# 256 rows of a rank scatter move from the SBUF path to row copies that GpSimd issues

## The chip, the cores and the metric

The kernel runs on one core of a Trainium2 chip. The metric is the device time of one execution in microseconds. The kernel before was timed three times; a separate execution was recorded by the hardware profiler, and all rows below are from that one.

## The reference

```python
B, N, D = 8, 2048, 2560
order = np.argsort(scores, axis=1)
ranks = np.argsort(order, axis=1)
out = np.zeros_like(x)
b_idx = np.arange(B)[:, None]
out[b_idx, ranks, :] = x
```

Each of 8 batches has 2048 rows of 2560 float32 values (10,240 bytes). A row's rank is the number of scores of its batch that come before its own, and the row is copied unchanged to that place in the output. So 168 MB are read and 168 MB are written, and nothing is computed on them; only the ranks are computed, from 64 KB of scores.

## The kernel before

**Ranks.** TensorE spreads the scores of a batch over all partitions (`broadcast`), VectorE counts for each row how many scores are smaller (`ranks`, the counting at line 317), and the sums become integer row numbers in `rank_i`. This goes batch by batch, in steps listed in `STEPS`.

**Groups of 256 rows through SBUF.** A batch has 8 groups of 256 rows; partition p of a group holds rows 2p and 2p+1. `BULK` lists the groups that go through SBUF. GpSimd issues all their transfers on one software queue: for group k one load into buffer k mod 8 (`load`: an indirect one at line 152, a plain one at line 165) and two scatters of 128 rows each (`scatter`, line 495). In the loop at the end GpSimd waits until the scatters of group k-4 are done, issues the load of group k+4, waits for load k and for the ranks of k, and issues the scatters of k. So some eight buffers are always between load and scatter, and the order of issue on GpSimd is the order of its queue.

**Rows that never enter SBUF.** Other rows are copied from HBM to HBM, one DMA for each row, since the target is known only as a number in a register. SyncE and ScalarE issue these DMAs on two hardware queues (`copy_rows`): a table of byte offsets is read into registers 32 at a time (line 446), then one DMA is issued for each row (line 456). `part` cuts the row into 2 x 2 pieces of 2,560 bytes, so that it runs on two of the core's 16 DMA engines. These rows are: all 256 of each group in `FULL`, half of the one in `HALF`, and *holes*.

**Holes.** In most groups some partitions are left out of load and scatter (`THIN`): their row numbers are pushed beyond the bounds, and the indirect DMA skips them. `WIDE_HOLE` is partitions 0 to 7 of 59 groups (16 rows each); `EXTRA` adds four partitions in four groups. For each distinct set of holes VectorE forms one column of `thin_row` at the start (reductions at lines 274 and 283); the first indirect load waits for it (`t_thin`). Before a buffer's first load with a hole, its partitions 0 to 7 are filled with zeros (`spare`: five times by ScalarE at line 217, once by GpSimd at line 511), so that nothing unwritten is read. In all 808 + 808 rows go through the two hardware queues.

**Offsets.** `rows_to_psum` turns ranks into one row with TensorE (line 378) and `to_bytes` makes byte offsets of them (line 389): for a copied group right after its ranks, for holes one batch later.

Of the kernel before, what the change touches and what calls it, by code (L numbers as in the profile page):

```python
# [7 lines left out]
P = 128  # L8
# [5 lines left out]
ENG = mybir.EngineType  # L14
# [26 lines left out]
def kernel(  # L41
# [6 lines left out]
    nc = tc.nc  # L48
    B, N, D = x.shape
    C = N // P  # L50
    ROW = 4 * D
# [2 lines left out]


    GROUPS = [(256 * i, 2) for i in range(8)]
    FULL = ((0, 0), (1, 0))
    HALF = ((2, 0),)
    MMAX = max(m for _, m in GROUPS)
    BULK = [(b, g) for b in range(B) for g in range(len(GROUPS)) if (b, g) not in FULL]  # L60
    NBUF = 8
# [1 line left out]


    PRIMED = {2: 'pool', 3: 'act', 4: 'act', 5: 'act', 6: 'act', 7: 'act'}
    WIDE_HOLE = (0, 8)
    EXTRA = {20: ((48, 4),), 30: ((44, 4),), 36: ((48, 4),), 52: ((48, 4),)}
    WHOLE = ()
    THIN = {
        key: (WIDE_HOLE, *EXTRA.get(k, ()))  # L70
        for k, key in enumerate(BULK)
        if key not in HALF and (k in PRIMED or k >= NBUF) and k not in WHOLE
    }

    HOLES = sorted(set(THIN.values()))
# [13 lines left out]
    def first_col(g):  # L89
# [9 lines left out]
    ident = pool.tile([P, P], F32, name="ident")  # L99
# [3 lines left out]
    rank = pool.tile([P, B * C], F32, name="rank")  # L103
# [4 lines left out]
    thin_row = pool.tile([P, len(HOLES)], I32, name="thin_row")  # L108
    copied = {k: 2 if k in FULL else 1 for k in FULL + HALF}
    full_i = {  # L110
        k: pool.tile([1, m * P], I32, name=f"full_i{k[0]}_{k[1]}") for k, m in copied.items()
    }
    thin_of = {b: [k for k in THIN if k[0] == b] for b in range(B)}
    thin_at = {}
    thin_n = {b: 0 for b in range(B)}
    for k, parts in THIN.items():
        thin_at[k] = thin_n[k[0]]
        thin_n[k[0]] += 2 * sum(n for _, n in parts)
    thin_i = {b: pool.tile([1, n], I32, name=f"thin_i{b}") for b, n in thin_n.items() if n}
    xb = [pool.tile([P, MMAX * D], F32, name=f"x{i}") for i in range(NBUF)]  # L120
    ps_all = psum.tile([P, N], F32, name="ps_all")
# [4 lines left out]
    out_bytes = out.rearrange("b n d -> (b n d)").bitcast(U8)  # L126
    x_bytes = x.rearrange("b n d -> (b n d)").bitcast(U8)

    with tc.tile_critical(no_gpsimd_drain=True):
        sp = Line(nc, nc.sync, "sp")  # L130
        act = Line(nc, nc.scalar, "act")
        pl = Line(nc, nc.gpsimd, "pool")
        dve = Line(nc, nc.vector, "dve")
# [3 lines left out]
        s_load = [nc.alloc_semaphore(f"load{i}") for i in range(NBUF)]  # L137
        s_scat = [nc.alloc_semaphore(f"scat{i}") for i in range(NBUF)]
        s_rows = {sp: nc.alloc_semaphore("rows_sp"), act: nc.alloc_semaphore("rows_act")}
        n_scat = [0] * NBUF  # L140

        n_load = [0] * NBUF
# [2 lines left out]
        def load(line, k, sem):  # L145
# [24 lines left out]
            if k:  # L170
# [13 lines left out]
                out=ident[:],  # L184
                in_=ident[:],
# [8 lines left out]
        for half in range(2):  # L194
# [3 lines left out]
                    out=part,  # L198
                    in_=part,
# [7 lines left out]


        def spare(k):
            return xb[k % NBUF][:WIDE_HOLE[1], :]  # L210

        t_primed = {}
        act.after(pl, t_ident)
        for k, who in PRIMED.items():
            if who == "act":
                t_primed[k] = act, act.did(
                    nc.scalar.copy(  # L217
                        out=spare(k),
                        in_=ident[:WIDE_HOLE[1], P - 1:].to_broadcast([WIDE_HOLE[1], MMAX * D]),
                    )  # L220
                )

# [3 lines left out]
        for g, (r, m) in enumerate(GROUPS):  # L226
            for j in range(m):
# [3 lines left out]
                        out=ps_col[:, B * c:B * (c + 1)],  # L231
                        in_=s_in[:, r + j:r + m * P:m],
# [6 lines left out]
                out=s_col[:].rearrange("p c b -> p (c b)"), in_=ps_col[:, :B * C]  # L239
# [6 lines left out]
        def broadcast(b):  # L246
            pe.after(dve, t_copied)
            ticks = []
            for c in range(C):
# [12 lines left out]
        t_rows = {}  # L262
# [5 lines left out]
                out=below[:], in_=mask[:, MMAX, :], axis=mybir.AxisListType.X, op=OP.add  # L268
            )
        )  # L270
        for i, parts in enumerate(HOLES):
            for n, (first, width) in enumerate(parts):
                dve.did(
                    nc.vector.tensor_reduce(
                        out=edge[:, n:n + 1],
                        in_=ident[:, first:first + width],
                        axis=mybir.AxisListType.X,
                        op=OP.add,
                    )
                )  # L280
            dve.after(dve, dve.n)
            dve.did(
                nc.vector.tensor_reduce(
                    out=hole[:, i:i + 1],
                    in_=edge[:, :len(parts)],
                    axis=mybir.AxisListType.X,
                    op=OP.add,
                )
            )
            dve.after(dve, dve.n)  # L290
        dve.did(
            nc.vector.tensor_scalar(
                out=hole[:], in0=hole[:], scalar1=float(N), scalar2=None, op0=OP.mult
# [6 lines left out]
                    out=thin_row[:], in0=hole[:], scalar1=below[:], scalar2=None, op0=OP.add  # L300
# [82 lines left out]
                    )  # L383
            dve.after(pe, pe.n)

        def to_bytes(out, b, g, first, n, m=2):
            lo = first_col(g)
            return dve.did(
                nc.vector.tensor_scalar(  # L389
                    out=out.rearrange("o (j i) -> o j i", j=m),  # L390
                    in0=ps_row[:1, P * lo:P * (lo + m)].rearrange("o (j p) -> o j p", j=m)[
                        :, :, first:first + n
                    ],
                    scalar1=float(b * N),
                    scalar2=float(ROW),
                    op0=OP.add,
                    op1=OP.mult,
                )
            )

        def thin_to_bytes(b):
            if thin_of[b]:
                rows_to_psum(thin_of[b])
            for k in thin_of[b]:
                at = thin_at[k]
                for first, width in THIN[k]:
                    t_rows[b] = to_bytes(
                        thin_i[b][:, at:at + 2 * width], b, k[1], first, width
                    )
                    at += 2 * width  # L410

        for b in range(B):
            dve.after(dve, dve.n)
            for q in range(4):
# [3 lines left out]
                        out=s_all[:, 512 * q:512 * (q + 1)],  # L418
                        in_=ps_all[:, 512 * q:512 * (q + 1)],
# [42 lines left out]
        def row_of(b, g, j, p):  # L462
            return b * N + GROUPS[g][0] + 2 * p + j

        for b in range(B):
            jobs = []
            for g in range(len(GROUPS)):
                if (b, g) in copied:
                    rows = [row_of(b, g, j, p) for j in range(copied[b, g]) for p in range(P)]
                    jobs.append((full_i[b, g], rows, t_rows[b, g]))  # L470
            rows = [
                row_of(b, g, j, p)
                for _, g in thin_of[b]
                for first, width in THIN[b, g]
                for j in range(2)
                for p in range(first, first + width)
            ]
            if rows:
                jobs.append((thin_i[b], rows, t_rows[b]))
            for table, rows, tick in jobs:  # L480
                half = len(rows) // 2
                copy_rows(sp, ENG.SP, b, table, 0, rows[:half], tick)
                copy_rows(act, ENG.Activation, b, table, half, rows[half:], tick)
# [4 lines left out]
        def scatters_done(line, k):  # L488
            line.wait(s_scat[k % NBUF], 16 * n_scat[k % NBUF])

        def scatter(k, j):
            b, g = BULK[k]
            col = b * C + first_col(g) + j
            n_scat[k % NBUF] += 1
            nc.gpsimd.indirect_dma_start(  # L495
                out=out_flat,
                out_offset=bass.IndirectOffsetOnAxis(ap=rank_i[:, col:col + 1], axis=0),
                in_=xb[k % NBUF][:, j * D:(j + 1) * D],
                in_offset=None,
                element_offset=b * N * D,  # L500
                **(dict(bounds_check=N - 1, oob_is_err=False) if (b, g) in THIN else {}),
            ).then_inc(s_scat[k % NBUF], 16)

        def load_ahead(k):
            i = k % NBUF
            load(pl, k, s_load[i])
            loaded[k] = (s_load[i], 16 * n_load[i])

        for k in range(1, NBUF):
            if PRIMED.get(k) == "pool":  # L510
                t_primed[k] = pl, pl.did(nc.gpsimd.memset(spare(k), 0.0))  # L511
            if k in t_primed:
                pl.after(*t_primed[k])
            load_ahead(k)
        for k, (b, g) in enumerate(BULK):
            if k >= LAG and k + NBUF - LAG < len(BULK):
                scatters_done(pl, k - LAG)
                load_ahead(k + NBUF - LAG)
            pl.wait(*loaded[k])
            pl.after(dve, t_bulk[b, g])  # L520
            for j in range(copied.get((b, g), 0), GROUPS[g][1]):
                scatter(k, j)
        for k in range(max(0, len(BULK) - NBUF), len(BULK)):
            scatters_done(pl, k)

        nc.gpsimd.dma_reset()

# [29 lines left out]
```

## Time and profile before

| | |
|---|---|
| median of 3 runs | 761.94 us (761.61 to 762.33) |
| the profiled execution | 761.48 us, of which the span is 759.8 us |
| busy share of the span | VectorE 55%, GpSimd 25%, TensorE 7%, ScalarE 3% |
| DMA queues: share of 16 engines | software queue 93.0%, hardware queues 3.8% and 2.9% |
| HBM | 177.83 MB read, 177.77 MB written |

The share of a DMA queue is the sum of the times of its packets over 16 times the span. A packet is one piece of data, or the 4 bytes by which a transfer reports that it is done. Packets that follow each other on one engine may overlap slightly in these records, so shares can add up to a little over 1.

### The profile page before, as it was taken

How to read it: one execution, taken by the hardware profiler on the slowest of the kernel's cores; microseconds unless marked ns; L12 is line 12 of the kernel's file. 1: busy time of each engine (PE TensorE's matmuls, PEld its weight loads, DVE VectorE, ACT ScalarE, POOL GpSimd, SP SyncE). 2: the span in 40 equal slices, each digit the busy share in tenths (PEclk: the TensorE clock that was granted, in tenths of full speed). 3: DMA queues.
4: the chain of work that ended last, by engine and by line, in shares of the span. 5: the costliest groups of instructions: out<-in, count | busy, mean ns of one | idle time of the engine just before them, and what ended most of it. 6: DMA issues, size and time to landing. Idle time of an engine off the chain costs nothing.

```text
span 759.8 us, 5293 instructions
## 1 busy us (share of the span) xinstructions
PE 55.3 (7%) x268; PEld 40.6 (5%) x268; DVE 419.9 (55%) x957; ACT 23.2 (3%) x6; POOL 189.6 (25%) x194
## 2 busy tenths in 40 slices
PE   3101001203003003003001002000000000000000
PEld 3101000102002002002000001000000000000000
DVE  6999998998998997998998990000000000000000
ACT  9200000000000000000000000000000000000000
POOL 5224222221321313133131322213131322312210
PEclk8555555555555555556555556555555555555555
DMA  8999999999999999999999999999999999999996
GB/s 360 427 412 427 423 422 427 424 421 433 424 422 429 426 431 424 429 428 424 428 424 431 426 428 428 426 430 425 431 423 431 424 429 426 425 427 425 421 406 292
DMA packets 36647, 319.43 MB, mean 420 GB/s; under 512 B 7664, under 2 KB 7664, under 8 KB 14128
## 3 DMA queue, kind: packets, MB, share of 16 engines
q0 software_dynamic: 26624, 299.84, 93.0%
q1 hardware_dynamic: 5136, 10.97, 3.8%
q10 hardware_dynamic: 4848, 8.28, 2.9%
q14 instruction: 37, 0.30, 0.1%
q8 instruction: 2, 0.03, 0.0%
HBM read 177.83 MB, written 177.77 MB: 468 GB/s over the span
## 4 chain that ended last, share of the span: by engine, by line
DMA 47%; DVE 42%; issue 3%; PE 3%; POOL 2%; POOLq 0%; SPq 0%
DMA out_dram<-x,rank_i 41%; DVE trash L317 36%; DMA x<-in_x_dram,thin_row 6%; PE ps_row L378 2%; DVE s_all L417 2%; DVE rank_i L364 1%; POOL out_dram L495 1%; DVE thin_i L389 0%; POOL x L152 0%; DVE rank_i L355 0%; DMA s_in<-in_scores_dram 0%; DVE rank L349 0%; DVE rank L343 0%; PE ps_row L230 0%; DVE full_i L389 0%
## 5 line engine op out<-in xcount | busy, mean ns | idle before, releaser
L317 DVE TENSOR_SCALAR_CACHE_REDUCE trash<-s_all,s_col 128x1792 bf16<-128x1792 f32 (+7 forms) x240 | 315.2, 1348 | 4.6
L152 POOL DMA_INDIRECT x<-in_x_dram,thin_row x59 | 61.3, 1039 | 445.3 <-DMA out_dram<-x,rank_i 262.5
L495 POOL DMA_INDIRECT out_dram<-x,rank_i x123 | 120.6, 981 | 86.2 <-issue 36.4
L317 DVE SCALAR_TENSOR_TENSOR trash<-s_all,s_col,mask 128x256 bf16<-128x256 f32 x128 | 61.6, 481 | 0.0
L378 PE MATMUL ps_row<-ident,rank 128*1 128x128 f32 x124 | 26.0, 390 | 343.4 <-DVE rank_i L364 287.3
L378 PEld LDWEIGHTS ps_row<-ident,rank 128*1 128x1 f32 x124 | 13.2, 113 | 355.5 <-DVE rank_i L364 290.0
L251 PE MATMUL ps_all<-ident,s_col 128*128 128x128 f32 x128 | 27.6, 405 | 58.3 <-DVE s_all L417 58.0
L251 PEld LDWEIGHTS ps_all<-ident,s_col 128*128 128x128 f32 x128 | 25.5, 219 | 60.6 <-DVE s_all L417 60.0
L217 ACT COPY x<-ident 8x5120 f32<-8x5120 f32 x5 | 21.9, 4453 | 0.0
L417 DVE COPY s_all<-ps_all 128x512 f32<-128x512 f32 x32 | 20.0, 684 | 0.3
L317 DVE DVE_READ_ACCUMULATOR trash<-s_all,s_col 128x1 f32 x240 | 19.9, 83 | 0.0
L389 DVE TENSOR_SCALAR thin_i<-ps_row 1x16 int32<-1x16 f32 (+1 forms) x63 | 5.7, 153 | 25.0 <-PE ps_row L378 25.0
L364 DVE TENSOR_SCALAR rank_i<-rank,hole 128x2 int32<-128x2 f32 x59 | 13.9, 236 | 2.1
L317 DVE DVE_READ_ACCUMULATOR trash<-s_all,s_col,mask 128x1 f32 x128 | 10.6, 83 | 0.0
L511 POOL MEMSET x<- 8x5120 f32 x1 | 4.4, 4354 | 0.0
L165 POOL DMA_DIRECT2D x<-in_x_dram x2 | 1.5, 736 | 8.6 <-DMA out_dram<-x,rank_i 8.6
L355 DVE CAST rank_i<-rank 128x4 int32<-128x4 f32 (+3 forms) x17 | 3.1, 185 | 0.6
L349 DVE TENSOR_TENSOR rank<-rank,acc 128x4 f32<-128x4 f32 (+3 forms) x17 | 2.8, 167 | 0.6
L343 DVE TENSOR_TENSOR rank<-acc,acc 128x4 f32<-128x4 f32 (+3 forms) x17 | 2.8, 166 | 0.6
L238 DVE COPY s_col<-ps_row 128x128 f32<-128x128 f32 x1 | 0.3, 292 | 4.8 <-PE ps_row L230 4.8
L230 PE MATMUL ps_row<-ident,s_in 8*128 8x8 f32 x16 | 2.1, 261 | 4.0 <-DMA s_in<-in_scores_dram 4.0
L389 DVE TENSOR_SCALAR full_i<-ps_row 1x256 int32<-1x256 f32 (+1 forms) x3 | 1.1, 368 | 2.0 <-PE ps_row L378 2.0
(16 smaller groups left out, 7.4 us busy)
## 6 DMA issues: line engine op xcount, KB each, us to landing
out_dram<-in_x_dram SPq DMA_DIRECT2D x808, 10.0 KB
out_dram<-in_x_dram ACTq DMA_DIRECT2D x808, 10.0 KB
x<-in_x_dram SPq DMA_DIRECT2D x1, 2560.0 KB, 12.7
x<-in_x_dram POOLq DMA_DIRECT2D x1, 2560.0 KB
out_dram<-x,rank_i POOLq DMA_INDIRECT x123
x<-in_x_dram POOLq DMA_DIRECT2D x1, 1280.0 KB, 40.5
x<-in_x_dram,thin_row POOLq DMA_INDIRECT x59, 41.4
s_in<-in_scores_dram SPq DMA_DIRECT2D x1, 64.0 KB
```

Of the source, the lines that this page charges most:

```text
L152: nc.gpsimd.indirect_dma_start(out=xb[k % NBUF][:, :m * D], out_offset=None, in_=x.rearrange("b (q j) d -> (b q) (j d)", j=m), in_offset=b ...
L217: nc.scalar.copy(out=spare(k), in_=ident[:WIDE_HOLE[1], P - 1:].to_broadcast([WIDE_HOLE[1], MMAX * D]),)
L251: nc.tensor.transpose(out=ps_all[:, P * c:P * (c + 1)], in_=s_col[:, c, b:b + 1].to_broadcast([P, P]), identity=ident[:],)
L317: do(out=trash[i][:, :P * (hi_c - lo_c)], in0=s_all[:, P * lo_c:P * hi_c], accum_out=acc[i][:, col:col + 1], **how,)
L343: nc.vector.tensor_tensor(out=rank[:, cols], in0=acc[0][:, cols], in1=acc[1][:, cols], op=OP.add)
L355: nc.vector.tensor_copy(out=rank_i[:, cols], in_=rank[:, cols])
L364: nc.vector.tensor_scalar(out=rank_i[:, cols], in0=rank[:, cols], scalar1=hole[:, i:i + 1], scalar2=None, op0=OP.add,)
L378: nc.tensor.transpose(out=ps_row[:1, P * c:P * (c + 1)], in_=rank[:, b * C + c:b * C + c + 1], identity=ident[:],)
L389: nc.vector.tensor_scalar(out=out.rearrange("o (j i) -> o j i", j=m), in0=ps_row[:1, P * lo:P * (lo + m)].rearrange("o (j p) -> o j p", j= ...
L417: nc.vector.tensor_copy(out=s_all[:, 512 * q:512 * (q + 1)], in_=ps_all[:, 512 * q:512 * (q + 1)],)
L495: nc.gpsimd.indirect_dma_start(out=out_flat, out_offset=bass.IndirectOffsetOnAxis(ap=rank_i[:, col:col + 1], axis=0), in_=xb[k % NBUF][:, ...
L511: t_primed[k] = pl, pl.did(nc.gpsimd.memset(spare(k), 0.0))
```

## The change

Group 4 of batch 1 (256 rows) leaves `BULK`, which now has 61 groups. Its rows are copied from HBM to HBM by GpSimd: one DMA for each row, a contiguous run of 10,240 bytes that is cut over all 16 DMA engines, 640 bytes on each. They go on GpSimd's software queue, six behind the scatters of a group, from group number 12 on; the offsets are read into GpSimd's registers 18 at a time. At the end GpSimd also waits for these rows.

A hole may now have a step (always 1 here). Groups 3, 4 and 5 of batch 0 (numbers 2, 3 and 4 of `BULK`) get a second hole, partitions 32 to 39, whose rows go to SyncE and ScalarE; `spare` fills 40 partitions in place of 8. The four older extra holes keep their numbers in `BULK`, and so three of them stand in the next group than before. The hardware queues now have 1,648 rows in place of 1,616.

```diff
-    FULL = ((0, 0), (1, 0))
+    FULL = ((0, 0), (1, 0), (1, 4))
     HALF = ((2, 0),)
+    BY_POOL = ((1, 4),)
+    POOL_FIRST, POOL_ROWS, POOL_LOADED = 12, 6, 18
...
-    WIDE_HOLE = (0, 8)
-    EXTRA = {20: ((48, 4),), 30: ((44, 4),), 36: ((48, 4),), 52: ((48, 4),)}
+    PRIMED_TO = 40
+    WIDE_HOLE = (0, 8, 1)
+    EXTRA = {2: ((32, 8, 1),), 3: ((32, 8, 1),), 4: ((32, 8, 1),), 20: ((48, 4, 1),), 30: ((44, 4, 1),), 36: ((48, 4, 1),), 52: ((48, 4, 1),)}
...
         def spare(k):
-            return xb[k % NBUF][:WIDE_HOLE[1], :]
+            return xb[k % NBUF][:PRIMED_TO, :]
...
-                if (b, g) in copied:
+                if (b, g) in copied and (b, g) not in BY_POOL:
                     rows = [row_of(b, g, j, p) for j in range(copied[b, g]) for p in range(P)]
                     jobs.append((full_i[b, g], rows, t_rows[b, g]))
...
+        pool_todo = [
+            (b, g, n, row_of(b, g, n // P, n % P))
+            for b, g in BY_POOL
+            for n in range(copied[b, g] * P)
+        ]
...
+        def pool_rows():
+            for b, g, n, row in pool_todo[:POOL_ROWS]:
+                pl.after(dve, t_rows[b, g])
+                if not pool_at:
+                    _, at = nc.values_load_multi_w_load_instructions(
+                        full_i[b, g][:, n:min(n + POOL_LOADED, copied[b, g] * P)],
+                        engines=[ENG.Pool],
...
+                    )
+                    pool_at.extend(at)
+                nc.gpsimd.dma_start(
+                    out=out_bytes[bass.ds(pool_at.pop(0), ROW)],
+                    in_=x_bytes[bass.ds(row * ROW, ROW)],
+                ).then_inc(s_pool_rows, 16)
+            del pool_todo[:POOL_ROWS]
...
             for j in range(copied.get((b, g), 0), GROUPS[g][1]):
                 scatter(k, j)
+            if k >= POOL_FIRST:
+                pool_rows()
+        assert not pool_todo
         for k in range(max(0, len(BULK) - NBUF), len(BULK)):
             scatters_done(pl, k)
+        pl.wait(s_pool_rows, 16 * pool_n)
```

## Rows read from the trace of the kernel before

**Rows 1.** The page: the span, and the DMA engines' busy tenths in 40 slices.
```profile
span 759.8 us, 5293 instructions
DMA  8999999999999999999999999999999999999996
```

**Rows 2.** Windows view: stretches from start and end; DMA share 1.00 means 16 engines.
```profile
core 0: us, PE busy (x) PEld busy (x) DVE busy (x) ACT busy (x) POOL busy (x), PEclk, DMA share, GB/s
4.00:20.00 16.00, 8.42 (x45) 7.84 (x46) 12.74 (x29) 16.00 (x5) 8.02 (x5) 0.81 1.01 429
200.00:400.00 200.00, 21.77 (x101) 15.59 (x102) 184.55 (x416) 0.00 (x0) 51.24 (x51) 0.53 1.01 427
...
735.00:750.00 15.00, 0.00 (x0) 0.00 (x0) 0.00 (x0) 0.00 (x0) 0.00 (x0) 0.50 0.97 400
750.00:754.00 4.00, 0.00 (x0) 0.00 (x0) 0.00 (x0) 0.00 (x0) 0.00 (x0) 0.50 0.89 376
754.00:757.00 3.00, 0.00 (x0) 0.00 (x0) 0.00 (x0) 0.00 (x0) 0.00 (x0) 0.50 0.30 126
757.00:760.00 3.00, 0.00 (x0) 0.00 (x0) 0.00 (x0) 0.00 (x0) 0.00 (x0) 0.50 0.03 10
```

**Rows 3.** The page: the chain that ended last, shares of the span by engine.
```profile
DMA 47%; DVE 42%; issue 3%; PE 3%; POOL 2%; POOLq 0%; SPq 0%
```

**Rows 4.** The page: DMA queues; packets, bytes, share of 16 engines' span.
```profile
q0 software_dynamic: 26624, 299.84, 93.0%
q1 hardware_dynamic: 5136, 10.97, 3.8%
q10 hardware_dynamic: 4848, 8.28, 2.9%
q14 instruction: 37, 0.30, 0.1%
```

**Rows 5.** Timeline of GpSimd, one late group: start, duration, what, idle before.
```profile
637.01 1.04 POOL L152 DMA_INDIRECT x<-in_x_dram,thin_row  x1 [8.59 <-DMA out_dram<-x,rank_i]
638.35 0.98 POOL L495 DMA_INDIRECT out_dram<-x,rank_i  x1 [0.30 <-issue]
639.64 0.97 POOL L495 DMA_INDIRECT out_dram<-x,rank_i  x1 [0.30 <-issue]
649.19 1.03 POOL L152 DMA_INDIRECT x<-in_x_dram,thin_row  x1 [8.57 <-DMA out_dram<-x,rank_i]
```

**Rows 6.** Tile view of the output: row copies; ns min/median/max, first and last start.
```profile
L456 SPq DMA_DIRECT2D out_dram<-in_x_dram x808: 613/631/2077, 20.5 to 742.7; - x162
L456 ACTq DMA_DIRECT2D out_dram<-in_x_dram x808: 623/633/2000, 20.6 to 748.0; - x162
```

**Rows 7.** The page: groups of instructions; busy us, mean ns, idle before.
```profile
L165 POOL DMA_DIRECT2D x<-in_x_dram x2 | 1.5, 736 | 8.6 <-DMA out_dram<-x,rank_i 8.6
L389 DVE TENSOR_SCALAR full_i<-ps_row 1x256 int32<-1x256 f32 (+1 forms) x3 | 1.1, 368 | 2.0 <-PE ps_row L378 2.0
L511 POOL MEMSET x<- 8x5120 f32 x1 | 4.4, 4354 | 0.0
```

**Rows 8.** Lines view: groups that the page leaves out; the same columns.
```profile
L274 DVE TENSOR_REDUCE edge<-ident 128x1 f32<-128x8 f32 (+1 forms) x5 | 0.6, 153 | 0.1
L180 POOL MEMSET mask<- 128x512 f32 x1 | 0.5, 528 | 0.0
```

**Rows 9.** View of line 446: offsets into registers; ns min/median/max.
```profile
L446 SPq TENSOR_LOAD <-full_i x10: 2065/4258/6757, 18.4 to 371.3; - x10
```

**Rows 10.** The page: DMA issues, the last number us from issue to landing.
```profile
x<-in_x_dram,thin_row POOLq DMA_INDIRECT x59, 41.4
```

**Rows 11.** Timelines: a scatter that waited for ranks, and ranks and scatters around 110 us.
```profile
37.90 0.96 POOL L495 DMA_INDIRECT out_dram<-x,rank_i  x1 [9.33 <-DVE rank_i L364]
...
109.58 0.75 DVE L364 TENSOR_SCALAR rank_i<-rank,hole 128x2 int32<-128x2 f32 x3
...
118.91 0.98 POOL L495 DMA_INDIRECT out_dram<-x,rank_i  x1 [0.30 <-issue]
```

More of the change, by code (lines that the diff above doesn't have):

```diff
@@ L65 @@
     PRIMED = {2: 'pool', 3: 'act', 4: 'act', 5: 'act', 6: 'act', 7: 'act'}
-    WIDE_HOLE = (0, 8)
-    EXTRA = {20: ((48, 4),), 30: ((44, 4),), 36: ((48, 4),), 52: ((48, 4),)}
+    PRIMED_TO = 40
+    WIDE_HOLE = (0, 8, 1)
+    EXTRA = {2: ((32, 8, 1),), 3: ((32, 8, 1),), 4: ((32, 8, 1),), 20: ((48, 4, 1),), 30: ((44, 4, 1),), 36: ((48, 4, 1),), 52: ((48, 4, 1),)}
     WHOLE = ()
     THIN = {
-        key: (WIDE_HOLE, *EXTRA.get(k, ()))
+        key: (() if k in WHOLE else (WIDE_HOLE,)) + EXTRA.get(k, ())
         for k, key in enumerate(BULK)
-        if key not in HALF and (k in PRIMED or k >= NBUF) and k not in WHOLE
+        if key not in HALF and (k in PRIMED or k >= NBUF) and (k in EXTRA or k not in WHOLE)
     }
@@ L117 @@
         thin_at[k] = thin_n[k[0]]
-        thin_n[k[0]] += 2 * sum(n for _, n in parts)
+        thin_n[k[0]] += 2 * sum(n for _, n, _ in parts)
     thin_i = {b: pool.tile([1, n], I32, name=f"thin_i{b}") for b, n in thin_n.items() if n}
@@ L139 @@
         s_rows = {sp: nc.alloc_semaphore("rows_sp"), act: nc.alloc_semaphore("rows_act")}
+        s_pool_rows = nc.alloc_semaphore("rows_pool")
         n_scat = [0] * NBUF
@@ L218 @@
                         out=spare(k),
-                        in_=ident[:WIDE_HOLE[1], P - 1:].to_broadcast([WIDE_HOLE[1], MMAX * D]),
+                        in_=ident[:PRIMED_TO, P - 1:].to_broadcast([PRIMED_TO, MMAX * D]),
                     )
@@ L271 @@
         for i, parts in enumerate(HOLES):
-            for n, (first, width) in enumerate(parts):
+            for n, (first, width, step) in enumerate(parts):
                 dve.did(
@@ L275 @@
                         out=edge[:, n:n + 1],
-                        in_=ident[:, first:first + width],
+                        in_=ident[:, first:first + width * step:step],
                         axis=mybir.AxisListType.X,
@@ L384, in rows_to_psum, with to_bytes @@
             dve.after(pe, pe.n)
-        def to_bytes(out, b, g, first, n, m=2):
+        def to_bytes(out, b, g, first, n, m=2, step=1):
             lo = first_col(g)
@@ L391, in to_bytes @@
                     in0=ps_row[:1, P * lo:P * (lo + m)].rearrange("o (j p) -> o j p", j=m)[
-                        :, :, first:first + n
+                        :, :, first:first + n * step:step
                     ],
@@ L405, in thin_to_bytes @@
                 at = thin_at[k]
-                for first, width in THIN[k]:
+                for first, width, step in THIN[k]:
                     t_rows[b] = to_bytes(
-                        thin_i[b][:, at:at + 2 * width], b, k[1], first, width
+                        thin_i[b][:, at:at + 2 * width], b, k[1], first, width, step=step
                     )
@@ L473 @@
                 for _, g in thin_of[b]
-                for first, width in THIN[b, g]
+                for first, width, step in THIN[b, g]
                 for j in range(2)
-                for p in range(first, first + width)
+                for p in range(first, first + width * step, step)
             ]
@@ L507, in load_ahead @@
             loaded[k] = (s_load[i], 16 * n_load[i])
+        pool_todo = [
[3 more added lines that the diff above has]
+        ]
+        pool_n = len(pool_todo)
+        pool_at = []
+        def pool_rows():
[5 more added lines that the diff above has]
+                        engines=[ENG.Pool],
+                        min_val=b * N * ROW,
+                        max_val=(b * N + N - 1) * ROW,
+                        skip_runtime_bounds_check_because=(
+                            "a rank counts other scores of one batch of N, so it lies in 0..N-1"
+                        ),
+                    )
[5 more added lines that the diff above has]
+            del pool_todo[:POOL_ROWS]
         for k in range(1, NBUF):
```

## The prediction, made before the result

> **What bounds the kernel now.** Four views answer this, in this order. First the slices of the page: the DMA engines are at nine tenths or more from the second slice to the last but one, in a span of 759.8 us [rows 1]. Second the windows: the DMA share is 1.01 between 4 and 20 us and again between 200 and 400 us, so all 16 engines are booked without a gap, while VectorE works for 184.55 of those 200 us and GpSimd for 51.24 [rows 2]. Third the chain that ended last: it puts 42% on VectorE [rows 3], and that must not be read as VectorE being the bound: the chain follows GpSimd's releases, and a release that comes later costs nothing as long as the engines have queued work. They have: a load lands a median 41.4 us after it was issued [rows 10], over three groups ahead. Fourth GpSimd's timeline late in the kernel: from one group's load to the next it is 649.19 - 637.01 = 12.18 us, of which GpSimd idles about 8.6 us for earlier scatters [rows 5]. So the bound is the time that the 16 DMA engines are occupied, and a change is worth what it takes from the fullest of them.
>
> Which are the fullest is seen at the end [rows 2]. From 750 to 754 us the share is 0.89, that is 14 engines of 16: two have no more work. ScalarE issued the last row copy at 748.0 [rows 6], and the code cuts each such copy over two engines; the two that are done are those. The other 14 stop around 754, a few of them later (share 0.30 from 754 to 757, 0.03 after). I call the two the row engines and the 14 the bulk engines. The idle booked to the end is 0.03 x 16 x 15 + 0.11 x 16 x 4 = 14 engine-us, plus some 3 us of each of the two while the bulk engines finish: about 10 us of slack on each row engine, none on the bulk engines.
>
> **What goes.** One group less through SBUF. In the steady state a group takes 12.18 us of every bulk engine [rows 5], and nothing else covers it: -12.18 us.
>
> **What comes: 256 rows in 640-byte pieces, one piece and one report of completion on each engine.** No row of before shows such a piece. Its price is built from the queues [rows 4]. The booked time of a queue is its share of 16 x 759.8 = 12,157 engine-us: 352.5 for q10 (2.9%; 4,848 packets, 8.28 MB) and 11,306 for q0 (93.0%; 26,624 packets, 299.84 MB). Let a packet cost a fixed time plus its bytes at a rate; the two queues then give 9.8 ns and 27.15 bytes per ns. With them a group, whose share on one engine is 8 load packets of 20,480 B, 16 scatter packets of 10,240 B and 3 reports (327,680 B in 27 packets), comes to 12.07 + 0.26 = 12.33 us, more than the 12.18 us that it takes: neighbouring packets overlap in the records, and (12.18 - 12.07) / 27 leaves 4.1 ns for a packet. A 640-byte piece is 23.6 ns of bytes, so piece and report are 23.6 + 2 x 4.1 = 31.8 ns by the period and 23.6 + 2 x 9.8 = 43.2 ns as booked. Times 256 rows that is 8.1 us and 11.1 us. The outer bounds: bytes alone, 6.0 us; and the price of a whole 2,560-byte piece with its part of the reports, 352.5 / 3,232 = 109 ns, so 27.9 us. I take 34 ns, 8.7 us, near the end that a real period gave; the point at which nothing is won is 12.18 / 256 = 47.6 ns.
>
> The rows say nothing on where a piece starts. [...]
>
> **Instructions.** They are fetched by DMA: 37 packets, 0.30 MB, some 0.1% or 12 us, 0.33 us a packet [rows 4]. 0.30 MB over 5,293 instructions [rows 1] is 57 B each; 256 rows at two instructions (offset and DMA) are 29 KB, 3.6 packets, 1.2 us if one engine fetches them all, 0.1 us spread over 16. I take 0.5 us.
>
> **The row engines.** They lose only half a group with the group that goes, because 8 of its 128 partitions were already a hole: 6.1 us. The three new holes take another three halves: 18.3 us. The hardware queues get 32 rows more; a row is booked with 352.5 / 808 = 436 ns, 218 ns on each of the two: +7.0 us. GpSimd's pieces: +8.7 us. Together -8.7 us, more than the bulk engines lose, so they stay off the path. That partitions 32 to 39 sit on the same two engines as 0 to 7 is in no row. [...] Without it the row engines would gain 9.6 us in place of losing 8.7, just their slack.
>
> **GpSimd.** In a group it is now busy until 640.61, that is 3.6 us after the load's start [rows 5]. Six DMAs more: a plain DMA takes 0.74 us in the mean for 128 and 256 pieces [rows 7], with the usual 0.30 us before each [rows 5]: 6 x 1.04 = 6.2 us at most for one of 16 pieces. The offsets are 15 reads of 18; SyncE's reads of 32 took 2.1 to 6.8 us, median 4.3 [rows 9]: 15 x 4.3 / 43 groups = 1.5 us. Sum 11.3 us of about 12.4 (12.18 and six times 34 ns): hidden in the wait of 8.6 us. What is queued behind these DMAs is the next load, and a late load is covered by the 41.4 us of queued work [rows 10].
>
> **VectorE and the start.** The two added edge reductions and one more sum delay `thin_row` by about 0.6 us (153 ns each and gaps [rows 8]); the engines are booked full from 4 us on by the first two plain loads [rows 2], so it costs nothing. Filling 40 partitions in place of 8: 8 x 5,120 took GpSimd 4,354 ns [rows 7], 128 x 512 528 ns [rows 8], both near 1 ns a column, so the time goes by columns: nothing. The new offsets of group (1, 4) cost 0.37 us and a wait of 0.67 us on TensorE [rows 7]. GpSimd waited for ranks only in the first groups (37.90); the group that moves up behind the removed one has its ranks by 110.3 and would be scattered near 118.9 [rows 11]: 8.6 us of cover against under 2 us of delay. SyncE and ScalarE take 0.63 us for a row [rows 6] and have 722 us for 824 rows and 26 reads, some 631 us.
>
> **Sum.** -12.18 + 8.7 + 0.5 = -3.0 us. The profiled execution took 761.48 us (span 759.8 and 1.7 around it), so 758.5 us; the median of the runs is 0.46 us above it: 758.9 us.
>
> **Rivals.**
> *The gain is eaten by small prices* (0.19, 760.4 to 763.4). Piece and report at the booked 43.2 ns, 11.1 us, and the instructions on one late engine, 1.2 us: -12.18 + 12.3 = +0.1 us, 762.0. For it: a few engines end late already [rows 2], and they set the end. Against it: the group's period is below its booked sum.
> *The report holds up the queue* (0.11, 763.5 to 778). Before, q0 sends one report for 8 or more pieces of 10 KB; now it has six pieces with a report each in a row, and on the bulk engines no other queue fills a pause. If pause, piece and report exceed 47.6 ns, the change loses 2.6 us for every 10 ns above; at the price of a whole 2,560-byte piece, 109 ns, it is +15.7 us, 777.7. Against it: reports of q1 and q10 come after every second piece, and share and packets of these queues leave no room for a pause.
> *The rows of SyncE and ScalarE end last* (0.05, about 767). ScalarE kept a pace of 727.4 / 808 = 0.90 us a row; at that pace 16 rows more put its last issue at 762.4, and with the 2.8 us that lie between the last bulk work and the span's end now the span would be 765.2, the time 767.4. It decides from (754 - 20.6) / 824 = 0.89 us a row on. Against it: the issue itself takes 0.63 us [rows 6], and the row engines get freer.
> *GpSimd falls behind* (0.03, over 765). It needs more than 12.4 + 41.4 / 43 = 13.4 us a group, that is 1.4 us for each DMA with its gap; indirect ones of 128 pieces take 0.98 and 0.30.
>
> **How the numbers follow.** The forecast, faster by 1.5 to 6 us, has 0.62. About 0.2%, 1.5 us, is what a measurement of this kernel can tell from no change: faster is below 760.4, slower above 763.5. Same has 0.19, slower 0.11 + 0.05 + 0.03 = 0.19. The range runs from 756.2 (a little inside the price of bytes alone: -12.18 + 6.0 is 755.8) to 763.5, where the slower cases begin. The forecast's own range is 756.2 to 760.4.
>
> **What will show it.** There will be 4,096 packets between 512 B and 2 KB. A group's period stays 12.18 us up to number 11 and is 12.3 to 12.4 us from then on; 12.5 would mean 50 ns a piece, and no gain. Six DMAs stand behind each pair of scatters on GpSimd, whose wait shrinks from 8.6 us to 1 to 5 us but doesn't vanish. ScalarE's last row is issued before 748, and the share at the end is 0.89 for longer. The prediction is wrong if the period rises by over 0.28 us, or if the last to finish is a row copy.

## The result and the profile after

The changed kernel took 770.62 us in the median of 4 runs (768.32 to 770.91), the kernel before 761.78: ratio 1.0109, 95% interval 1.0094 to 1.0125. Timed again beside other kernels it was 1.0119 (1.0103 to 1.0134). The forecast was 758.9 us, in a range from 756.2 to 763.5. The profiled execution took 768.32 us, 6.8 us more than that of before. A ratio, here and below, is estimated from the single runs without those that are over 1.5% above the fastest of their kernel, and so need not be the quotient of the medians.

The page of the changed kernel, parts 1 to 3:
```profile
span 766.7 us, 5884 instructions
...
DMA  8999999999999999999999999999999999999994
...
DMA packets 44604, 316.54 MB, mean 413 GB/s; under 512 B 11824, under 2 KB 15920, under 8 KB 22512
...
q0 software_dynamic: 34384, 296.58, 92.5%
q1 hardware_dynamic: 5232, 11.13, 3.9%
q10 hardware_dynamic: 4944, 8.44, 2.9%
```
The 4,096 pieces are there (15,920 - 11,824 packets between 512 B and 2 KB), and q0 moves 3.3 MB less than before [rows 4]. Yet its time is 0.925 x 16 x 766.7 = 11,347 engine-us against 11,306. Less data took more time. Part of that is the 7,760 packets more, 76 engine-us at the prediction's 9.8 ns each; but the 3.3 MB less are worth 120 engine-us at its 27.15 bytes per ns, so packets must also have got longer: in the packet records q0's packets of 20,480 B take 780 ns in the mean, before 767.

The windows of the changed kernel (columns as in [rows 2]):
```profile
200.00:400.00 200.00, 21.36 (x96) 15.13 (x97) 185.50 (x418) 0.00 (x0) 96.66 (x144) 0.52 1.01 419
...
735.00:750.00 15.00, 0.00 (x0) 0.00 (x0) 0.00 (x0) 0.00 (x0) 1.93 (x2) 0.50 0.97 403
750.00:754.00 4.00, 0.00 (x0) 0.00 (x0) 0.00 (x0) 0.00 (x0) 0.00 (x0) 0.50 0.84 356
754.00:757.00 3.00, 0.00 (x0) 0.00 (x0) 0.00 (x0) 0.00 (x0) 0.00 (x0) 0.50 0.52 222
757.00:760.00 3.00, 0.00 (x0) 0.00 (x0) 0.00 (x0) 0.00 (x0) 0.00 (x0) 0.50 0.35 150
760.00:767.00 7.00, 0.00 (x0) 0.00 (x0) 0.00 (x0) 0.00 (x0) 0.00 (x0) 0.50 0.15 61
```
Two things are to be seen here. In the middle the share is 1.01 as before while the rate fell from 427 to 419 GB/s: the engines are booked as full and move less. And the end is ragged: before, most of the 14 bulk engines stopped between 754 and 756 and none worked past 758; now some stop around 753, and between 757 and 760 five or six are still at work (0.35 x 16).

GpSimd's loads between 200 and 680 us, from the lines view (count of loads behind the x). First before, then after:
```profile
L152 POOL DMA_INDIRECT x<-in_x_dram,thin_row x40 | 41.7, 1042 | 337.7 <-DMA out_dram<-x,rank_i 221.7 <-DVE trash L317 89.5 <-DVE s_all L417 18.1
```
```profile
L156 POOL DMA_INDIRECT x<-in_x_dram,thin_row x38 | 40.6, 1068 | 189.9 <-DMA out_dram<-x,rank_i 122.4 <-DVE trash L321 53.9 <-DVE thin_i L393 7.0
```
40 loads against 38 in 480 us; by their starts, 12.08 us a group became 12.62. The forecast allowed 0.28 us more as the point where nothing is won.

GpSimd itself, one group of the changed kernel, and the row copies in the tile view (the last row is GpSimd's):
```profile
225.57 1.06 POOL L156 DMA_INDIRECT x<-in_x_dram,thin_row  x1 [6.05 <-DVE trash L321]
226.93 1.03 POOL L499 DMA_INDIRECT out_dram<-x,rank_i  x1 [0.30 <-issue]
228.26 0.98 POOL L499 DMA_INDIRECT out_dram<-x,rank_i  x1 [0.30 <-issue]
229.22 3.01 POOL L535 DMA_DIRECT2D out_dram<-in_x_dram  x6
237.27 1.07 POOL L156 DMA_INDIRECT x<-in_x_dram,thin_row  x1 [5.05 <-DVE s_all L421]
```
```profile
L460 SPq DMA_DIRECT2D out_dram<-in_x_dram x824: 3/631/1744, 20.9 to 748.1; - x165
L460 ACTq DMA_DIRECT2D out_dram<-in_x_dram x824: 623/624/1570, 20.9 to 735.2; - x165
...
L535 POOL DMA_DIRECT2D out_dram<-in_x_dram x256: 486/516/586, 147.7 to 672.0; - x128
```
The six DMAs take 3.0 us, and GpSimd still waits 5 to 6 us before a load, so it isn't late. SyncE's last row is issued at 748.1, long before the end. The bulk engines and their queue set the time.

**Where the time sits.** The trace also records each DMA packet. On a bulk engine six pieces and six reports follow each other every 34 ns (32 ns for each piece), the price taken. I followed each such train along its engine, 557 of them up to the second load packet, and averaged the durations by position:

```
packet behind the train of the changed kernel      mean ns   without a stall
1st load packet                                      762        761
2nd load packet                                      912        761    (460 of 557 over 790)
3rd to 8th load packet                            761 to 763    761
16 scatter packets                                385 to 386    385
```

The train costs its 6 x 34 = 204 ns, and then one later packet comes 151 ns late in the mean. The delay belongs to the engine: on those that could be followed over ten or more groups it is 280 to 340 ns each time on some, 60 to 130 ns on others, nearly none on a few. In 43 trains 0.3 us make 13 us, about the spread between the engines that end at 753 and those that end at 765.

### The profile page after: what moved, and what is told of

It reads as the page before. It is cut to its first block, busy times and chain, and to the rows that moved or that the text cites. A ratio compares the mean times of both kernels' runs of the same rounds, so it can differ in the third digit from the quotient of the medians.

```text
span 766.7 us, 5884 instructions
## 1 busy us (share of the span) xinstructions
PE 58.5 (8%) x268; PEld 41.9 (5%) x268; DVE 421.0 (55%) x962; ACT 23.2 (3%) x6; POOL 317.9 (41%) x447
## 2 busy tenths in 40 slices
DMA packets 44604, 316.54 MB, mean 413 GB/s; under 512 B 11824, under 2 KB 15920, under 8 KB 22512
## 4 chain that ended last, share of the span: by engine, by line
DMA 81%; DVE 6%; issue 5%; POOL 2%; POOLq 1%; PE 0%; SPq 0%
DMA out_dram<-x,rank_i 75%; DMA x<-in_x_dram,thin_row 6%; DVE trash L321 5%; POOL out_dram L499 1%; POOL x L156 1%; POOLq L525 1%; POOL out_dram L535 0%; DMA s_in<-in_scores_dram 0%; DVE s_all L421 0%; PE ps_row L234 0%; DVE rank_i L359 0%; DVE edge L278 0%; DVE rank L353 0%; DVE rank L347 0%; DVE hole L287 0%
## 5 line engine op out<-in xcount | busy, mean ns | idle before, releaser
L535 POOL DMA_DIRECT2D out_dram<-in_x_dram x256 | 128.4, 523 | 40.3 <-issue 39.6
L382 PE MATMUL ps_row<-ident,rank 128*1 128x128 f32 x124 | 28.3, 414 | 343.6 <-DVE rank_i L368 262.7
L221 ACT COPY x<-ident 40x5120 f32<-40x5120 f32 x5 | 21.9, 4453 | 0.0
L368 DVE TENSOR_SCALAR rank_i<-rank,hole 128x2 int32<-128x2 f32 x58 | 14.1, 244 | 2.1
L543 POOL MEMSET x<- 40x5120 f32 x1 | 4.4, 4397 | 0.0
```

What stands on the lines that cost most here:

```text
L221: nc.scalar.copy(out=spare(k), in_=ident[:PRIMED_TO, P - 1:].to_broadcast([PRIMED_TO, MMAX * D]),)
L368: nc.vector.tensor_scalar(out=rank_i[:, cols], in0=rank[:, cols], scalar1=hole[:, i:i + 1], scalar2=None, op0=OP.add,)
L382: nc.tensor.transpose(out=ps_row[:1, P * c:P * (c + 1)], in_=rank[:, b * C + c:b * C + c + 1], identity=ident[:],)
L535: nc.gpsimd.dma_start(out=out_bytes[bass.ds(pool_at.pop(0), ROW)], in_=x_bytes[bass.ds(row * ROW, ROW)],).then_inc(s_pool_rows, 16)
```

## The experiments

All are edits of the changed kernel unless said otherwise; times are medians, the ratio is to the kernel before on the same chip.

**Rows left out (e1), and rows and new holes left out (e13).**
```diff
-            if k >= POOL_FIRST:
-                pool_rows()
-        assert not pool_todo
...
-        pl.wait(s_pool_rows, 16 * pool_n)
# e13 also
-    EXTRA = {2: ((32, 8, 1),), 3: ((32, 8, 1),), 4: ((32, 8, 1),), 20: ((48, 4, 1),), ...
+    EXTRA = {20: ((48, 4, 1),), ...
```


> The 256 rows of group (1, 4) are left out of the output; the rest is the changed kernel. Theory A (the small rows cost time beyond their own pieces: six short pieces with six reports use up what an engine has fetched of its queue ahead, and a later packet of the next load comes late): one group less and nothing for it, 761.8 - 12.2 = 749.6 us. Theory B (the new holes, the shift of the old ones by a group or the longer row chains cost the time): 752 us or more.

> The 256 rows of group (1, 4) are left out of the output, and the three new holes are taken back, so that SyncE and ScalarE have 800 rows each. If the group is worth what its period says and only the row copies hid it: 749 to 752 us, with the bulk engines done near 745. If 755 us or more, the group was never worth 12.2 us.

e1: 763.54 us in the median of all ten runs (753.61 to 768.48), ratio 0.9963 (0.9929 to 0.9997) from the seven below 765; my number was missed by 14 us. SyncE's row copies and the windows of e1:
```profile
L460 SPq DMA_DIRECT2D out_dram<-in_x_dram x824: 3/631/1563, 20.6 to 759.3; - x165
```
```profile
735.00:750.00 15.00, 0.00 (x0) 0.00 (x0) 0.00 (x0) 0.00 (x0) 0.00 (x0) 0.50 0.54 215
750.00:754.00 4.00, 0.00 (x0) 0.00 (x0) 0.00 (x0) 0.00 (x0) 0.00 (x0) 0.50 0.05 13
```
By the packet records two engines are left at work at 745 (share 0.05 from 750 on), so the bulk engines were done some 12 us earlier, as the group's period says. But SyncE issued its last row at 759.3, and that set the time: the rival on row copies, seen here because nothing else was late. e13, with 800 rows a queue: 749.23 us (747.56 to 750.62), ratio 0.9825 (0.9807 to 0.9843); the last rows of both queues were issued at 744.5 and 744.8. So the group is worth 12.7 us, and 24 rows a queue more or less, with the holes that they come from, decide whether that is seen.

**New holes alone (e2), on the kernel before.**
```diff
-    FULL = ((0, 0), (1, 0), (1, 4))
+    FULL = ((0, 0), (1, 0))
-    BY_POOL = ((1, 4),)
+    BY_POOL = ()
```


> The kernel before with the three new holes (32 to 39) alone, all groups in BULK, no rows on GpSimd. Theory A: bulk engines untouched, 761.8 us within 1. Theory B: 765 us or more.

760.72 us (759.01 to 772.98, 10 runs), ratio 0.9977 (0.9961 to 0.9994). That is just under the band of theory A; on the kernel before, the holes are not the cause of 9 us. The spread is put down to the row copies again: in the profiled run (762.10 us) SyncE's last was issued at 756.7.

**Trains of three (e3, again e17).**
```diff
             for j in range(copied.get((b, g), 0), GROUPS[g][1]):
                 scatter(k, j)
-            if k >= POOL_FIRST:
-                pool_rows()
+                if k >= POOL_FIRST:
+                    pool_rows(POOL_ROWS // 2)
```


> The changed kernel with three rows behind each scatter in place of six behind the second. Theory A: six short descriptors leave long packets in what is fetched ahead, so that no packet comes late: the forecast's sum holds, 758 to 760 us. Rival C (each report of a small row holds its engine a little, however they are grouped): as the changed kernel, 770 us.

759.07 us (758.58 to 760.11), ratio 0.9957 (0.9941 to 0.9974). The same rows, pieces and reports, grouped by three, gave the forecast's sum. That ends rival C: a price of each report would not care for the grouping. Windows of the second run of this kernel:
```profile
735.00:750.00 15.00, 0.00 (x0) 0.00 (x0) 0.00 (x0) 0.00 (x0) 0.00 (x0) 0.50 0.95 394
750.00:754.00 4.00, 0.00 (x0) 0.00 (x0) 0.00 (x0) 0.00 (x0) 0.00 (x0) 0.50 0.36 151
754.00:757.00 3.00, 0.00 (x0) 0.00 (x0) 0.00 (x0) 0.00 (x0) 0.00 (x0) 0.50 0.05 20
```
Most bulk engines stop between 750 and 752.5, against 754 to 756 before: some 3.5 us earlier, as -12.18 + 8.7 has it.

**Rows between load and scatters (e4).**
```diff
+            if k >= POOL_FIRST:
+                pool_rows()
             for j in range(copied.get((b, g), 0), GROUPS[g][1]):
                 scatter(k, j)
-            if k >= POOL_FIRST:
-                pool_rows()
```


> The changed kernel with the six rows issued between a group's load and its scatters, so that a scatter follows them on the engines. Theory A: the first packet behind the train covers 0.38 us in place of 0.76, so a stall grows by up to 0.38 us in 43 groups: 780 to 787 us. Rival D (what comes late is the load's read from HBM, behind writes to HBM; a scatter reads SBUF): the stall goes, 758 to 760 us.

769.47 us (768.37 to 771.32), ratio 1.0091 (1.0073 to 1.0109): neither number. The packet records show the load packets at 761 to 762 ns now and the fourth scatter packet behind the train at 513 ns in place of 385. So the stall isn't one of reads from HBM (rival D is out), and it doesn't hit a packet of fixed number: in both cases the late packet is the one that ends 40 KB behind the train (two loads, or four scatters). Theory A, as a fixed number of entries fetched ahead, put 0.38 us too much on it; that an engine fetches entries ahead is the theory's own assumption, which no run shows.

**Other lengths of train (e7, e11).** `pool_rows((2, 4)[j])` and `pool_rows((1, 5)[j])` in the place of `pool_rows(POOL_ROWS // 2)`.

> Two rows behind the first scatter and four behind the second. Theory A: 8 short descriptors in a train; if the count that stalls lies between 8 and 12, as with three rows 759 us; if between 6 and 8, 762 to 766 us. Either is possible; rival C (each report costs by itself) was already against 759 us with three.

> One row behind the first scatter, five behind the second: 10 short descriptors in the longer train. Four in a train (8) ran without a stall, six (12) stalled for 0.15 us in the mean. Theory A: a threshold between 8 and 12, so between 759 us (none) and 765 us (about half the stall). In the trace the second load packet tells: 761 ns without a stall.

e7: 759.31 us (758.80 to 759.77), ratio 0.9966 (0.9952 to 0.9980). e11: 761.83 us (760.88 to 764.86), ratio 1.0003 (0.9990 to 1.0016). By packet records the second load packet is late by 2 ns behind four rows, 43 ns behind five, 151 ns behind six, always in the mean of the bulk engines.

**Fewer or more pieces (e5, e6, e9, e10).** e5 and e6 gave the DMA the shapes 4 x 2,560 and 32 x 320; e9 and e10 a pattern like that of `part`, which isn't contiguous (shown is e10; e9 has j=16 and ROW // 32):
```diff
-                    out=out_bytes[bass.ds(pool_at.pop(0), ROW)],
-                    in_=x_bytes[bass.ds(row * ROW, ROW)],
+                    out=out_bytes[bass.ds(pool_at.pop(0), ROW)].rearrange("(i j n) -> j i n", i=2, j=4, n=ROW // 8),
+                    in_=x_bytes[bass.ds(row * ROW, ROW)].rearrange("(i j n) -> j i n", i=2, j=4, n=ROW // 8),
```


> The changed kernel (six rows behind the second scatter) with each row in 4 pieces of 2,560 B in place of 16 of 640 B, still one DMA a row. Theory A (the count of short descriptors on an engine uses up what it has fetched ahead): an engine gets a quarter of the pieces; if every engine still gets a report for each row, 6 reports and 1.5 pieces in a train, under the 12 that stall, no late packet: 757 to 759 us. Theory E (six reports in a row, each waiting for a write, hold the packets behind): the reports are still six: 768 us. Should the four pieces always fall on the same four engines, these get 256 x 0.105 = 27 us for the 12.2 taken away: 777 us.

> The changed kernel with each row in 32 pieces of 320 B, two on each engine with one report: 18 short descriptors in a train in place of 12. Theory A: the stall grows with the count, by half or more of its 0.15 us mean and 0.33 us on the slowest engines, and the pieces cost 1 to 2 us more: 775 to 785 us. Theory E: six reports as now, only the pieces cost more: 771 to 773 us.

> The changed kernel with each row in 32 pieces of 320 B, now by an access pattern that isn't contiguous, two pieces and one report on each engine: 18 short descriptors in a train, still six reports. (The runs with 4 and with 32 pieces before had the same 4,096 packets of 640 B as the changed kernel: a contiguous pattern is cut into 16 whatever its shape, so they were two more runs of that kernel.) Theory A (the count of short descriptors): more stall behind a train, over 775 us. Theory E (reports in a row): only 1 to 2 us for the added pieces, 771 to 773 us.

> The changed kernel with each row on 4 engines, two pieces of 1,280 B on each. Theory A: if the four engines go round, an engine gets 3 pieces and 6 reports or fewer in a train, under the 12 that stall: 757 to 760 us. Theory E: six reports in a row remain if all 16 engines report: 768 us. If the four engines are always the same, these get 256 x 0.11 us for 12.2: 775 to 780 us.

Three of these are misses: e5, e6 and e9 have 4,096 packets of 640 B like the changed kernel, whatever the shape, and are further runs of it: 768.69, 769.12 and 768.78 us. Only e10 differs; its page:
```profile
DMA packets 44604, 316.56 MB, mean 411 GB/s; under 512 B 14896, under 2 KB 14896, under 8 KB 22512
```
No packets between 512 B and 2 KB, and 3,072 more below 512 B: the packet records have 1,024 pieces of 2,560 B on four engines a row, and on the other twelve a packet of 8 B each. It took 769.24 us (768.54 to 772.39), ratio 1.0088 (1.0069 to 1.0107), with 485 load packets over 790 ns, late by 183 ns in the mean, between 200 and 680 us (changed kernel: 510, by 194). So twelve entries stall although most of the packets have 8 bytes. What the pieces do change is the delay: on one engine trains with one 2,560-byte piece alternate with trains with two, and on eight of the ten engines that could be followed the median delay behind one piece is 99 to 111 ns longer than behind two (on the other two there is none behind two). The second piece itself takes 93 ns more than an 8-byte packet (102 against 9). So a train that takes longer leaves a shorter delay: the delay looks like the rest of a time that twelve entries need anyway, and not like a price on top of each; what in the engine takes that time isn't shown. Six packets and six reports were in every one of these trains, so whether the packets or the reports are what counts (A or E) was not separated.

**Without the new holes (e14 with sixes, e8 and e18 with threes).** The edit of `EXTRA` of e13.

> The changed kernel without the three new holes, trains of six. Theory A (the stall is the whole loss): 43 trains still stall, up to 0.33 us on the slowest engines, 768 to 771 us. If the holes are a good part of the loss: 765 us or less.

> Trains of three, and the three new holes (partitions 32 to 39) taken back, so that SyncE and ScalarE have 1,600 rows. If the new holes are needed (the row engines would end last): 761 us or more, and a row copy or a packet of these two engines is the last. If not: 758 to 759 us, since the bulk engines set the end; less spread between runs if the rows of SyncE end the slow ones.

e14: 766.80 us (766.63 to 767.12), ratio 1.0062 (1.0047 to 1.0078); outside both of my ranges, nearer the first. e8: 757.60 us (757.16 to 757.99), ratio 0.9943 (0.9926 to 0.9959), a little under the 758 to 759 expected. Three of the kernels once more, side by side:

> The changed kernel once more, beside the next two. 768 to 771 us as before.

> Trains of three with the new holes, once more. Theory A (the stall behind trains of six is the loss): 10 us under the changed kernel, 758 to 760 us.

> Trains of three without the new holes, once more. If the holes cost something: 1.5 us under the run before, 757.6 us; if the difference was that of the occasions: within 0.8 us of it.

770.41, 759.15 and 757.23 us; ratios 1.0119 (1.0103 to 1.0134), 0.9968 (0.9956 to 0.9980) and 0.9942 (0.9929 to 0.9956). Trains of three in place of six are worth 11.3 us, taking back the holes another 1.9 us. With sixes the holes cost more: 3.6 us by the medians of e16 and e14, which ran on different chips, 4.3 us by their ratios. At the start, first the changed kernel, then e18:
```profile
4.00:20.00 16.00, 8.09 (x44) 7.51 (x45) 12.69 (x32) 16.00 (x5) 8.42 (x5) 0.81 0.99 417
20.00:30.00 10.00, 1.26 (x8) 1.02 (x6) 9.79 (x24) 4.31 (x1) 4.16 (x4) 0.67 0.98 408
```
```profile
4.00:20.00 16.00, 8.10 (x45) 7.52 (x45) 12.95 (x29) 16.00 (x5) 8.22 (x5) 1.00 1.01 429
20.00:30.00 10.00, 1.43 (x7) 1.03 (x5) 9.79 (x24) 4.31 (x1) 3.96 (x4) 1.00 1.01 432
```
The holes take work from engines that have nothing else yet (0.98 against 1.01: some 10 engine-us idle up to 30 us, since the first piece of a row copy starts at 24.6 us), and hand it to the row queues later. In the packet records it is two engines that idle: from 16 to 19 us 14.1 are at work in the changed kernel, 16.1 in e18. How that becomes 1.9 us and more at the end of the bulk engines was not settled.

**More rows on GpSimd (e12, e15)**, without the new holes: group (1, 5) too, five rows behind each scatter; or half of group (3, 0), four behind each.
```diff
-    POOL_FIRST, POOL_ROWS, POOL_LOADED = 12, 6, 18
+    POOL_FIRST, POOL_ROWS, POOL_LOADED = 8, 10, 20     # e12; e15: 11, 8, 16
-    BY_POOL = ((1, 4),)
+    BY_POOL = ((1, 4), (1, 5))                         # also in FULL; e15: (3, 0), also in HALF
```


> Trains and no new holes as in the fastest run so far (757.6 us), but two groups, (1, 4) and (1, 5), as rows on GpSimd, five behind each scatter from group 8 on. If trains of five don't stall: another 12.2 - 256 x 0.034 = 3.5 us less on the bulk engines, 754 us. If they stall as sixes do, two trains a group lose 2 x 0.15 us in some 50 groups, more on the slowest engines: 770 us or more. The rows of SyncE and ScalarE, 784 each, should end before 741 us.

> The fastest version (trains of three, no new holes, 757.6 us) with four rows behind each scatter and 128 rows more on GpSimd, half of group (3, 0). Theory A: trains of four don't stall, the bulk engines lose half a group (6.1 us) and get 128 x 0.034 = 4.4 us: 1.7 us less, 755.9 us. If eight rows a group in two trains stall after all: 760 us or more.

769.68 us (769.53 to 771.21), ratio 1.0106 (1.0084 to 1.0127): fives stall twice a group, at the second load packet (+44 ns) and at the fourth scatter packet (+39 ns) in the mean. That mean hides the cause: most engines that could be followed have no delay at all, and three have 140 to 190 ns at each place, about 300 to 360 ns a group. Over 52 groups that is 15 to 19 us on the slowest engines, the 16 us by which the time lies above the 754 of no stall. e15: 759.23 us (758.81 to 759.53), ratio 0.9963 (0.9950 to 0.9977), 3.3 us above what I expected. About half of the bulk engines did stop earlier, by 750, but one or two ran until 755.6; which, and why, wasn't found. So e18 is the fastest kernel here.

## Why the prediction was wrong

*The bound* was right: the 16 DMA engines, the bulk engines above all.

*What goes, -12.18 us*: right; e13 gave -12.7.

*What comes, 34 ns a row and engine*: this is the step that failed. The size of the piece was right (34 was picked between 31.8 and 43.2, so to the nanosecond is partly luck), but the step priced the pieces as if nothing behind them changed. Six in a row cost 204 ns and then 151 ns more in the mean, up to 340 on the slowest engines: 59 to 91 ns a row in place of 34, above the 47.6 at which nothing is won. In whole times: without the new holes the 256 rows cost 17.6 us in sixes (e14 against e13) and 8.0 us in threes (e18 against e13, on different chips; 8.9 by the ratios), where the sum had 8.7. The evidence against a pause was read from q1 and q10 of the row engines, where a report comes after two pieces and the queues take turns (nine in ten q1 pieces of before are followed by a packet of q10); no row of before had twelve short entries in a row on one queue.

*The rival "the report holds up the queue"* had 0.11. Its place (six pieces and six reports in a row on the bulk engines) and its threshold were right; the pause sits in a packet further back, not between the pieces. The measured 770.62 us lies in its 763.5 to 778. It is right by place and size, not shown as to the report.

*The slowest engine.* The sum was made for a mean engine. The stall differs by engine from none to 0.34 us, and the kernel ends with the last.

*The row engines*: called off the path. In the changed kernel they are; but e1 shows that they stood only just below the surface, and the runs with and without the three holes that these cost 1.9 us with threes (e17, e18) and some 4 us with sixes (e16, e14), where the sum has nothing for them. The -8.7 us for these two engines took partitions 32 to 39 to lie on the same two as 0 to 7; no row of before shows that, and no run shows it directly, but the start fits it: with the new holes just two engines run dry from 16 to 19 us (14.1 at work in the changed kernel), while the hole of partitions 0 to 7 alone leaves none dry (16.1 in e18). Had the second hole lain on two other engines, these would have lost no more than the row engines lose to the first.

*GpSimd, VectorE, the instructions*: nothing in the runs speaks against them; six DMAs take GpSimd 3.0 us where 6.2 were allowed. The start was called full from 4 us on; with the new holes it is not (share 0.99 and 0.98). The instruction queue has 42 packets in place of 37 in the page.

*Where a piece starts*: the rows of before say nothing on it, and the price has no term for it. In the records of the changed kernel the 4,096 pieces take 32 ns at the tenth and at the ninetieth percentile, at a distance of 34: no difference by where a piece starts is seen.

## What to carry to other kernels

Price what a new kind of transfer does to the packets behind it, not its own bytes alone: try the same transfers in smaller groups before giving them up; here three at a time were worth 11.3 us against six. When engines in parallel set the end, a delay that differs between them counts at its largest: here up to 0.34 us a train, where the mean is 0.15. And ask which bound stands just behind the one that is being moved: 24 row copies a queue hid 12 us in e1.

## What the runs showed that was not expected

In these runs eight short entries (pieces and reports) in a row on GpSimd's queue delay a later packet by 2 ns in the mean (e7), ten by 43 ns (e11), twelve by 151 ns (the changed kernel). Each engine has its own delay, from nearly none to 340 ns behind twelve, and it shrinks by about as much as the train itself gets longer (e10: 99 to 111 ns less behind a train with 93 ns more). The delay falls on the second packet when the next ones are 20 KB loads (912 ns in place of 761), and on the fourth when they are 10 KB scatters (e4: 513 in place of 385). A 10,240-byte row issued by GpSimd was cut into 16 x 640 B with each of the three other shapes that were tried (4,096 such packets in e5, e6 and e9); e10's pattern over four engines gave packets of 8 B to the other twelve, and these trains delayed what followed as well, by 183 ns in the mean of the packets over 790 ns.
